# Rotary products read from PSUM, key-value latents three steps apart, top-k rounds moved to later stages: a layer with indexed sparse attention and latent attention on one core

## The chip, the core and the metric

The kernel runs on one core of one Trainium2 chip. The metric is the device time of one execution in microseconds. The core's engines run side by side and synchronize by semaphores: TensorE (PE, matrix products and transposes, which write the accumulator memory PSUM, eight banks of 128 rows by 512 fp32 columns), VectorE (DVE), ScalarE (ACT), GpSimd (POOL, which only works on SBUF here) and SyncE (SP, which issues the DMAs). Each engine works through its own queue in order: an instruction that waits holds up all that stand behind it on its engine.

## What is computed

One layer for 512 tokens of width 1024, in fp32:

```python
xn = rms_norm(h, norm_gain)
proj = xn @ w_in
(q_a, k_a, v_a, g_a, q_i, k_i, w_i, c_q, c_kv, k_rope, g_b) = split(proj)
# group A: 8 heads of 64; each query attends to 128 keys chosen by an indexer
q_i = [rope(q_i[..., :32]), q_i[..., 32:]]        # 8 index heads of 64
k_i = [rope(k_i[:, :32]), k_i[:, 32:]]            # one index key of 64
score[t, s] = sum_h w_i[t, h] * relu(q_i[t, h] . k_i[s]) * scale
sel = top_k(where(admissible, score, -1e30), 128)
o_a = softmax(rope(rms(q_a)) . rope(rms(k_a))[sel]) @ v_a[sel]
# group B: latent attention, 8 heads of 96
q_b = rms(c_q) @ w_uq
k_nope, v_b = split(rms(c_kv) @ w_ukv)
o_b = chunk_causal_softmax(rms(q_b), rms([k_nope, k_rope])) @ v_b
h = h + [o_a * silu(g_a), o_b * silu(g_b)] @ w_out
```

A query may read the keys of its own chunk of 64 tokens and of the chunks before it.

## The kernel before, in words

**Numbers as pairs.** Each matrix operand is a sum of a rounded high part and a low part. `mm3` (line 180) makes three matmuls of such pairs: high by high, low by high, high by low. One *step* of a projection is one `mm3` over 128 rows of the contraction, three matmuls of 512 columns.

**Order of the work.** PE's order is the order of the program (line 90); the other engines' queues are put in order when the kernel is built, by a planner with a cost model that prefers what comes earlier in the program among what it takes to be ready. A stage is a generator that yields after every step; `weave` (line 161) advances several of them in proportion to the numbers that it is given, and on a tie the one listed first. `later` (line 133) makes a function due a number of nanoseconds after now, by a clock of modelled matmul times (line 125), and `tick` starts what is due between two steps. `LAG_SMALL`, `LAG_QI` and `LAG_KI` are such numbers.

**Weights.** `wt` (line 275) has the pieces of the weights loaded eight ahead of use: a DMA into a buffer `wst` (three of them), the high part by ACT (line 267), the low part by POOL or DVE (line 270), into nine buffers each. `first` (line 226) keeps ACT's casts of weights beyond a number of pieces ahead behind a given instruction.

**Projections.** `tok_jobs` (line 291) and `feat_jobs` (line 301) make a list of jobs, one for each output tile; a job has `nk` steps into one PSUM bank and a function `use` that is called after its last step. `stream` (line 311) sets the order of the steps. Job i begins `nk / group` places behind job i - 1; with `skew` true it stays so, and with `skew` false its start is rounded down to a multiple of `nk`, so that with two jobs of eight steps in a group of two both start together, alternate, and end one after the other.

**The stages**, in order:

1. x is scaled, transposed and split (line 339), and the index keys, index weights and rotary key are projected (`small_step`, line 479). `use_small` (line 423) copies the result to SBUF; its `turn` transposes it into one PSUM bank `p`, ACT copies that to `sm` (line 431) and scales the index weights in it (line 432), DVE makes the two rotary products from `sm` (lines 438, 439), adds them twice (line 441) and copies the unrotated half twice (line 442); `turn2` transposes the keys and splits them into `KIH` and `KIL` (line 448, by `split`, line 416).
2. Index queries of token tiles 1, 2 and 3 (`qi_`, line 485). `use_qi` (line 503) copies the bank `a` to SBUF with ACT (line 507), DVE makes the rotary products from that copy (`rope_mul`, lines 410 and 413) and adds them in place (line 509); `turn` transposes and splits (lines 517, 520).
3. `lkv` (line 561): two key-value latents of eight steps. `latent` (line 455) takes squares and the high part with ACT (lines 460, 461) and the low part with DVE (line 462). The first nine steps run alone, the other seven are woven with five steps of `index` (line 531).
4. `lq`: three query latents, woven with the other 19 steps of `index`. A step of it makes one head's scores in a bank `sc` or `tr`, two of each, ACT applies relu in the bank (line 541), and DVE adds it, weighted, to `acc` (lines 544, 546), which frees the bank.
5. Top-k: `topk` (line 549) has 48 steps, 16 rounds for each of three token tiles. A step finds eight maxima (MAX8, line 554) and strikes them out (MATCH_REPLACE8, line 555), both on DVE, behind the DVE instruction last noted in `dve[0]`; after the 48th, three instructions (line 558) make masks. `TK` (line 64) says how many steps go with which stage: the end of `lq` (5), the first gates of group B (5), the first up-projection (5), the second (14), attention B (10), the stage with the projections of k_a (4); the last 5 go with the stage after that.
6. The up-projections `up(0)` and `up(1)` (line 671), each woven with 12 steps of gates. Their tiles use two banks `sc`; ACT evacuates (lines 637 to 639, 660, 661), and DVE's line 642 is the last reader of a key-value tile's bank.
7. Attention B (line 810) with the gate and q_a projections (line 874), the k_a projection, whose `use` ends with a product on DVE (line 831), and v_a.
8. Attention A (line 901), whose line 694 adds the masks to the scores and frees their bank, with the output projection.

Of the kernel before, what the change touches and what calls it, by code (L numbers as in the profile page):

```python
# [11 lines left out]
AF = mybir.ActivationFunctionType  # L12
# [5 lines left out]
NT = S // 128  # L18
# [38 lines left out]
KEEP_QI = 5  # L57
# [3 lines left out]
KEEP_EXP = 4  # L61
KEEP_UP = 4

TK = (5, 5, 5, 14, 10, 4)
I0, I1, I2 = 9, 5, 20
B1, B2, B3, B4 = 84, 23, 11, 7
A0, A1, OA = 2, 62, 18
# [17 lines left out]
def layer(ctx: ExitStack, tc: tile.TileContext, x, norm_gain, w_in, a_q_norm, a_k_norm, b_q_latent,  # L85
          b_kv_latent, w_uq, w_ukv, b_q_norm, b_k_norm, w_out, cst, out):
    nc = tc.nc
# [12 lines left out]
    def tmp(shape=(128, 512)):  # L100
        return sb("tmp", shape)
# [124 lines left out]
    def first(ins, m):  # L226

        for c in copies[used[0] + 1 + m:]:
            after(c, ins)
# [71 lines left out]
    def feat_jobs(name, nk, rh, rl, tiles, use):  # L301

        def job(c, m):
            def step(a, k):
                h, l = name(k) if callable(name) else wt(name, k)
                mm3(a[:m], h[:, c:c + m], l[:, c:c + m], rh(k), rl(k), k == 0, k == nk - 1)
            return nk, step, lambda a: use((c, m), a)

        return [job(c, m) for c, m in tiles]

    def stream(jobs, group=2, banks=("mm",), skew=True):

        order, start = [], 0
        for i, (nk, _, _) in enumerate(jobs):
            s = start if skew else start - start % nk
            order += [(s + k, i, k) for k in range(nk)]
            start += nk / group
        acc = {}
        for _, i, k in sorted(order):
            nk, step, use = jobs[i]  # L320
            if k == 0:
                acc[i] = psum(banks[i % len(banks)])
            step(acc[i], k)
            if k == nk - 1:
                use(acc.pop(i))
            yield 1
# [49 lines left out]
    cs32 = P.tile([128, 2, NT, 32], F32, name="cs32")  # L376
# [30 lines left out]
    def rope_mul(m1, m2, src, tab, t, heads, d):  # L407

        h = d // 2
        nc.vector.tensor_tensor(  # L410
            halves(m2), halves(src)[:, :, ::-1, :],
            tab[:, 1, t].rearrange("p (s d) -> p s d", s=2)[:, None].to_broadcast([128, heads, 2, h]), op=OP.mult)
        nc.vector.tensor_tensor(m1, src, tab[:, 0, t][:, None, :].to_broadcast([128, heads, d]), op=OP.mult)
# [5 lines left out]
    sm = P.tile([128, NT, 104], F32, name="sm")  # L419
# [3 lines left out]
    def use_small(_, a):  # L423
        st = tmp()
        nc.scalar.copy(st[:104], a[:104])

        def turn():
            p = psum("tr")
            for t in range(NT):
                transpose(p[:, t * 104:t * 104 + 104], st[:104, tok(t)], ident[:104, :104])  # L430
            nc.scalar.copy(sm.rearrange("p t c -> p (t c)"), p[:, :416])
            nc.scalar.activation(sm[:, :, 96:104], sm[:, :, 96:104], AF.Copy, scale=512 ** -0.5)

            kid = tmp((128, NT, 128))
            k4 = kid.rearrange("p t (u d) -> p t u d", u=2)
            m = tmp((128, 2, NT, 32))
            src = sm[:, :, 32:64]
            nc.vector.tensor_tensor(m[:, 0], src, cs32[:, 0], op=OP.mult)
            nc.vector.tensor_tensor(halves(m[:, 1]), halves(src)[:, :, ::-1, :], halves(cs32[:, 1]), op=OP.mult)
            for u in range(2):  # L440
                nc.vector.tensor_tensor(k4[:, :, u, 0:32], m[:, 0], m[:, 1], op=OP.add)
                nc.vector.tensor_copy(k4[:, :, u, 32:64], sm[:, :, 64:96])

            def turn2():
                p = psum("tr")
                for t in range(NT):
                    transpose(p[:, tok(t)], kid[:, t], ident)
                split(KIH, KIL, p)
            later(LAG_KI, turn2)
        later(LAG_SMALL, turn)  # L450
# [52 lines left out]
    def use_qi(t, a):  # L503
        q = tmp()
        q3 = q.rearrange("p (h d) -> p h d", h=8)
        m = tmp((128, 8, 32))
        first(nc.scalar.copy(q, a), KEEP_QI)
        rope_mul(q3[:, :, 0:32], m, q3[:, :, 0:32], cs32, t, 8, 32)
        nc.vector.tensor_tensor(q3[:, :, 0:32], q3[:, :, 0:32], m, op=OP.add)

        def turn():
            p = psum("tr")
            for h in range(4):
                transpose(p[:, tok(h)], q[:, tok(h)], ident)
            p3 = p.rearrange("p (h c) -> p h c", h=4)
            for u in range(2):
                nc.scalar.copy(QI[u][HALF[u], :, tok(t - 1)], p3[HALF[u]])
            for u in range(2):
                a, b = QI[u][HALF[u], :, tok(t - 1)], QI[u][HALF[1 - u], :, tok(t - 1)]
                nc.vector.tensor_tensor(b, p3[HALF[u]], f32(a), op=OP.subtract)  # L520
        later(LAG_QI, turn)
# [36 lines left out]
            nc.vector.tensor_scalar(masks[t], masks[t], -2e38, NEG, op0=OP.is_gt, op1=OP.mult)  # L558

    ix = index()  # L560
    lkv = stream(feat_jobs("c_kv", 8, xh, xl, [(0, 128), (128, 128)], lat_kv), 2, ("pv", "mm"), False)
    lq = stream(feat_jobs("c_q", 8, xh, xl, [(0, 128), (128, 128), (256, 128)], lat_q), 3, ("mm",), True)
    run(take(lkv, I0))
    weave((lkv, 16 - I0), (take(ix, I1), I1))
# [52 lines left out]
    src = sm[:, :, 0:32]  # L617
# [348 lines left out]
```

## Time and profile before

| | |
|---|---|
| median of 3 runs | 345.5 us (345.32 to 345.57) |
| the profiled execution | 345.63 us, span 343.8 us |
| PE busy | 326.7 us (95%) |
| DVE busy | 265.5 us (77%) |
| ACT busy | 219.6 us (64%) |
| POOL busy | 182.2 us (53%) |
| granted TensorE clock | 0.998 |

The profile is of one execution. Times are microseconds from the start of the span. A row of a timeline gives start, duration, engine, line, operation, the tiles out<-in, the shape and, in brackets, how long the engine had been idle before and which instruction's end released it. A row "x2" joins two instructions that follow each other. Matmuls are pipelined and overlap in the records, so PE's pace is read from start to start. A row of groups gives the count, the total busy time and the mean duration in nanoseconds; a row of one line's forms gives the least, median and greatest duration in nanoseconds, then the first and the last start; a row of a stretch gives its length and then the busy time of PE, of PE's weight loads, of DVE, ACT and POOL, the granted clock, and the DMA share and rate.

### The profile page before, as it was taken

The page shows a single profiled execution, that of the slowest core. Times are in us where ns is not written, and L with a number is a line of the kernel's source. Part 1 is how long each engine was busy: PE and PEld are TensorE (multiplying, and loading weights), DVE is VectorE, ACT ScalarE, POOL GpSimd, SP SyncE. Part 2 cuts the span into 40 slices and gives each one's busy share as a digit, 9 for nine tenths or more (in the row PEclk, how much of TensorE's full clock was granted, in tenths as well). Part 3 has the DMA queues.
Part 4 walks back from the last instruction along what each step waited for, and adds up shares of the span by engine and source line. Part 5 has one row for each costly group of instructions (what it writes and reads, how often), then busy time and mean ns, then how long its engine had stood idle before and what let it go on. Part 6 is the DMA issues. An engine that isn't in the chain of part 4 may idle for free.

```text
span 343.8 us, 5465 instructions
## 1 busy us (share of the span) xinstructions
PE 326.7 (95%) x1688; PEld 271.9 (79%) x1688; DVE 265.5 (77%) x634; ACT 219.6 (64%) x536; POOL 182.2 (53%) x193
## 2 busy tenths in 40 slices
PE   2999899999899999999999999999999999999995
PEld 2887787888688788788888788888888788788884
DVE  4925787759999797877779987679898776877466
ACT  4934558574757776878876898434526988878210
POOL 1745462166697998315623469519924635457100
PEclk9999999999999999999999999999999999999999
DMA  7753344124032433103320055515697324410006
GB/s 267 196 151 98 84 132 126 29 94 122 2 99 71 113 92 102 54 2 92 92 64 0 1 128 159 144 24 141 170 212 216 126 79 137 120 66 0 2 0 244
DMA packets 28806, 34.83 MB, mean 101 GB/s; under 512 B 5341, under 2 KB 16874, under 8 KB 28778
## 3 DMA queue, kind: packets, MB, share of 16 engines
q1 hardware_dynamic: 28202, 33.57, 34.7%
q10 hardware_dynamic: 576, 0.92, 0.7%
q8 instruction: 13, 0.21, 0.3%
q14 instruction: 15, 0.12, 0.1%
HBM read 27.14 MB, written 2.10 MB: 85 GB/s over the span
## 4 chain that ended last, share of the span: by engine, by line
PE 49%; DVE 17%; POOL 11%; DMA 8%; issue 6%; ACT 6%; SPq 1%; POOLq 0%; DVEq 0%; ACTq 0%
PE mm L126 28%; PE sc L126 7%; DMA wst<-in_w_in 7%; PE pv L126 6%; PE tr L130 5%; POOL wl L270 4%; POOL sml L216 4%; DVE acc L555 2%; DVE ob L923 2%; DVE m L554 2%; PE mm L130 2%; DVE z L694 2%; ACT wh L267 2%; ACT z L696 1%; DVE wl L270 1%
## 5 line engine op out<-in xcount | busy, mean ns | idle before, releaser
L270 POOL TENSOR_TENSOR wl<-wst,wh 128x512 fp32r<-128x512 f32 (+2 forms) x79 | 98.3, 1253 | 59.3 <-ACT wh L267 47.9
L267 ACT CAST wh<-wst 128x512 fp32r<-128x512 f32 (+2 forms) x89 | 50.9, 586 | 30.2 <-DMA wst<-in_w_in 22.0
L126 PE MATMUL mm<-wh,xh 128*128 128x512 f32 x120 | 50.2, 419 | 0.0
L126 PE MATMUL mm<-wl,xh 128*128 128x512 f32 x120 | 47.6, 397 | 0.2 <-POOL wl L270 0.2
L126 PE MATMUL mm<-wh,xl 128*128 128x512 f32 x120 | 47.4, 395 | 0.0
L216 POOL TENSOR_TENSOR sml<-sml,nhalf 128x4 f32<-128x4 f32 (+2 forms) x28 | 32.0, 1149 | 25.9 <-ACT sml L825 14.8
L696 ACT ACTIVATE z<-z,sml 128x256 f32<-128x256 f32 (+2 forms) x64 | 35.9, 561 | 11.1 <-DVE sml L694 10.0
L713 POOL TENSOR_SCALAR z<-z,sml 128x512 f32<-128x512 f32 (+2 forms) x32 | 18.2, 570 | 41.6 <-DVE sml L709 31.4
L126 PE MATMUL mm<-xh,wh 128*128 128x512 f32 x80 | 33.3, 417 | 0.0
L126 PE MATMUL mm<-xl,wh 128*128 128x512 f32 x80 | 31.7, 396 | 0.0
L126 PE MATMUL mm<-xh,wl 128*128 128x512 f32 x80 | 31.6, 395 | 0.0
L126 PEld LDWEIGHTS mm<-wh,xl 128*128 128x128 f32 x120 | 22.6, 188 | 5.3
L554 DVE MAX8 m<-acc 128x8 f32<-128x512 f32 (+2 forms) x48 | 26.3, 549 | 0.0
L555 DVE MATCH_REPLACE8 acc<-m,acc 128x512 f32<-128x512 f32 (+2 forms) x48 | 25.9, 540 | 0.0
L126 PEld LDWEIGHTS mm<-wl,xh 128*128 128x128 f32 x120 | 22.8, 190 | 3.5 <-POOL wl L270 0.5
L126 PEld LDWEIGHTS mm<-wh,xh 128*128 128x128 f32 x120 | 22.7, 189 | 3.0
L694 DVE CUSTOM_DVE_ANT_0 z<-sc,wide,nqb 128x512 f32<-128x512 f32 (+3 forms) x32 | 17.4, 543 | 6.4 <-PE sc L126 6.2
L416 DVE TENSOR_TENSOR pl<-tr,ph 128x512 fp32r<-128x512 f32 (+1 forms) x32 | 17.6, 551 | 5.9 <-ACT ph L416 5.6
L416 ACT CAST ph<-tr 128x512 fp32r<-128x512 f32 (+1 forms) x32 | 15.2, 474 | 8.0 <-PE tr L130 7.6
L126 PE MATMUL sc<-kl,bhl 96*128 96x512 f32 (+3 forms) x96 | 20.2, 322 | 0.0
L126 PEld LDWEIGHTS sc<-kl,bhl 96*128 96x128 f32 x96 | 16.6, 189 | 3.2 <-DVE bhl L794 0.3
L923 DVE TENSOR_TENSOR ob<-mm,ob 128x512 f32<-128x512 f32 (+1 forms) x25 | 16.5, 667 | 2.9 <-PE mm L126 2.6
(214 smaller groups left out, 884.6 us busy)
## 6 DMA issues: line engine op xcount, KB each, us to landing
wst<-in_w_in SPq DMA_DIRECT2D x48, 256.0 KB, 2.7
wst<-in_w_out SPq DMA_DIRECT2D x16, 256.0 KB, 2.9
xin<-in_x SPq DMA_DIRECT2D x4, 512.0 KB, 4.1
k_a<-tmp SPq DMA_DIRECT2D x16, 128.0 KB, 3.5
ob<-in_x SPq DMA_DIRECT2D x8, 256.0 KB, 4.5
wst<-in_w_in SPq DMA_DIRECT2D x8, 192.0 KB, 2.6
wst<-in_w_uq SPq DMA_DIRECT2D x6, 192.0 KB, 2.3
wst<-in_w_in SPq DMA_DIRECT2D x8, 128.0 KB, 2.1
```

The lines of the kernel that those rows point to most:

```text
L126: nc.tensor.matmul(o, l, r, start=start, stop=stop)
L130: nc.tensor.transpose(o, i, idn)
L216: nc.gpsimd.tensor_tensor(dst, src, nhalf[:, :src.shape[-1]], op=OP.pow)
L267: copies.append(nc.scalar.copy(h, st))
L270: i = E(eng).tensor_tensor(l, st, f32(h), op=OP.subtract)
L416: return nc.scalar.copy(h, p), nc.vector.tensor_tensor(l, p, f32(h), op=OP.subtract)
L554: nc.vector.max(m, masks[t])
L555: dve[0] = nc.vector.match_replace(masks[t], m, masks[t], -3e38).ins
L694: m = nc.vector.tensor_tensor_reduce(z, sc[:, :n], mask(t), nq(h, t), 3e38, OP.add, OP.min, r[:, i:i + 1])
L696: e = nc.scalar.activation(z, z, AF.Exp, bias=r[:, i:i + 1], scale=-1.0, accum_out=r[:, 2 + i:3 + i])
L713: nc.gpsimd.tensor_scalar(z, z, w, 0.0, op0=OP.mult, op1=OP.add)
L923: nc.vector.tensor_tensor(o, p[:, :n], o, op=OP.add)
```

## The change

- `TK`: the first and second up-projection take 4 and 9 top-k steps in place of 5 and 14, attention B takes 13 in place of 10, and the stage with k_a 7 in place of 4. The sum of the six numbers is 43 as before.
- `stream` takes a number for `skew`: then each job starts that many places behind the one before. `lkv` gets 3: its first latent ends with the 12th of 16 steps, the second with the 16th.
- Index keys: DVE's rotary products read the PSUM bank, ACT copies the unrotated half out of the same bank twice in place of DVE's copies, and the scaling of the index weights stands behind all that.
- Index queries: ACT copies only the unrotated half of each head, and `rope_mul` reads the PSUM bank.

```diff
-TK = (5, 5, 5, 14, 10, 4)
+TK = (5, 5, 4, 9, 13, 7)
...
-            start += nk / group
+            start += nk / group if skew in (True, False) else skew
...
             nc.scalar.copy(sm.rearrange("p t c -> p (t c)"), p[:, :416])
-            nc.scalar.activation(sm[:, :, 96:104], sm[:, :, 96:104], AF.Copy, scale=512 ** -0.5)
+            p3 = p[:, :416].rearrange("p (t c) -> p t c", t=NT)
...
-            src = sm[:, :, 32:64]
+            for u in range(2):
+                nc.scalar.copy(k4[:, :, u, 32:64], p3[:, :, 64:96])
+            src = p3[:, :, 32:64]
...
             for u in range(2):
                 nc.vector.tensor_tensor(k4[:, :, u, 0:32], m[:, 0], m[:, 1], op=OP.add)
-                nc.vector.tensor_copy(k4[:, :, u, 32:64], sm[:, :, 64:96])
+            nc.scalar.activation(sm[:, :, 96:104], sm[:, :, 96:104], AF.Copy, scale=512 ** -0.5)
...
-        first(nc.scalar.copy(q, a), KEEP_QI)
-        rope_mul(q3[:, :, 0:32], m, q3[:, :, 0:32], cs32, t, 8, 32)
+        a3 = a.rearrange("p (h d) -> p h d", h=8)
+        first(nc.scalar.copy(q3[:, :, 32:64], a3[:, :, 32:64]), KEEP_QI)
+        rope_mul(q3[:, :, 0:32], m, a3[:, :, 0:32], cs32, t, 8, 32)
...
-    lkv = stream(feat_jobs("c_kv", 8, xh, xl, [(0, 128), (128, 128)], lat_kv), 2, ("pv", "mm"), False)
+    lkv = stream(feat_jobs("c_kv", 8, xh, xl, [(0, 128), (128, 128)], lat_kv), 2, ("pv", "mm"), 3)
```

## The prediction

> **What bounds the kernel now.** I read the page first, then the timeline of the matrix engine (PE), then the timelines of VectorE (DVE), ScalarE (ACT) and GpSimd (POOL) around each place where PE stood still, and last the stretches by stage.
>
> ```profile
> span 343.8 us, 5465 instructions
> PE 326.7 (95%) x1688; PEld 271.9 (79%) x1688; DVE 265.5 (77%) x634; ACT 219.6 (64%) x536; POOL 182.2 (53%) x193
> L554 DVE MAX8 m<-acc 128x8 f32<-128x512 f32 (+2 forms) x48 | 26.3, 549 | 0.0
> L555 DVE MATCH_REPLACE8 acc<-m,acc 128x512 f32<-128x512 f32 (+2 forms) x48 | 25.9, 540 | 0.0
> ```
>
> PE is busy nearly throughout, so nothing can be won but the places where it stands. A top-k step costs DVE 549 + 540 = 1089 ns, 1.09 us. In PE's timeline:
>
> ```profile
> 33.50 0.40 PE L126 MATMUL mm<-wl,xh 128*128 128x512 f32 x1
> 33.74 0.39 PE L126 MATMUL mm<-wh,xl 128*128 128x512 f32 x1
> 35.07 0.63 PE L130 MATMUL tr<-ident,tmp 128*128 128x128 f32 x4 [0.94 <-DVE tmp L509]
> 42.47 0.65 PE L130 MATMUL tr<-ident,tmp 128*128 128x128 f32 x4 [0.29 <-DVE kil L416]
> 59.83 0.44 PE L126 MATMUL tr<-kih,qi 128*128 128x384 f32 x1 [0.77 <-DVE acc L546]
> 89.43 0.50 PE L126 MATMUL sc<-wh,lath 128*128 128x512 f32 x1 [0.31 <-DVE vb L642]
> 95.25 0.45 PE L126 MATMUL sc<-wh,lath 128*128 128x384 f32 x1 [1.39 <-DVE vb L642]
> 116.33 0.44 PE L126 MATMUL sc<-wh,lath 128*128 128x384 f32 x1 [0.28 <-DVE vb L642]
> 143.92 0.66 PE L130 MATMUL tr<-ident,z 128*128 128x128 f32 x4 [0.26 <-ACT z L715]
> 158.97 0.42 PE L130 MATMUL pv<-ident,qst 128*96 128x128 f32 x2 [0.19 <-DVE tmp L746]
> ```
>
> Matmuls of 512 columns start 0.23 us apart when nothing is late (33.50 to 33.74). The first stop therefore costs 35.07 - 33.74 - 0.23 = 1.10 us, 0.16 more than the idle time in its bracket (the pipeline fills again). I add 0.16 to the next five as well: 0.45, 0.93, 0.47, 1.55 and 0.44. These six stops, 4.94 us, lie in the stages that are edited, and each ends on DVE.
>
> **The change part by part. The rotary products.** What the stop at 35.07 waits for is this chain, on ACT and then on DVE:
>
> ```profile
> 30.22 0.50 ACT L431 COPY sm<-tr 128x416 f32<-128x416 f32 x1
> 31.19 0.58 ACT L507 COPY tmp<-mm 128x512 f32<-128x512 f32 x1
> 35.73 1.17 ACT L517 CAST qi<-tr 64x512 fp32r<-64x512 f32 x2 [2.04 <-PE tr L130]
> ```
>
> ```profile
> 30.76 0.53 DVE L438 TENSOR_TENSOR tmp<-sm,cs 128x128 f32<-128x128 f32 x1 [3.06 <-ACT sm L431]
> 31.41 0.91 DVE L442 COPY tmp<-sm 128x128 f32<-128x128 f32 x2
> 32.24 1.03 DVE L441 TENSOR_TENSOR tmp<-tmp 128x128 f32<-128x128 f32 x2
> 33.20 0.41 DVE L410 TENSOR_TENSOR tmp<-tmp,cs 128x256 f32<-128x256 f32 x1
> 36.94 1.39 DVE L520 TENSOR_TENSOR qi<-tr,qi 64x512 fp32r<-64x512 f32 x2 [2.01 <-ACT qi L517]
> 41.72 0.69 DVE L416 TENSOR_TENSOR kil<-tr,kih 128x512 fp32r<-128x512 f32 x1
> ```
>
> Reading PSUM directly doesn't free DVE from ACT. The first L520 subtracts rows 0 to 63 and needs only the first L517, yet both L520 start at 36.94, as the second L517 ends (35.73 + 1.17 = 36.90): an access of a PSUM bank by DVE is queued behind ACT's accesses ahead of it in the program. So L438 will wait for L431 and for the two new ACT copies of the keys. The price of such a copy out of PSUM, 128 columns wide:
>
> ```profile
> 83.90 0.27 ACT L589 ACTIVATE tmp<-tr 128x128 f32<-128x128 f32 x1
> ```
>
> Two copies of 0.27 after L431 (end 30.72), overlapping a little as ACT's instructions do, put L438 at about 31.1, 0.35 later than now. The two L442 leave DVE (0.83 from start to start), and L438 has one operand in PSUM, so that its 0.53 can come down to the 0.28 of this shape; that is 0.25 more. L410 then starts at 33.20 + 0.35 - 0.83 - 0.25 = 32.5, and the query's copy ahead of it, half as wide, now lasts between 0.27 and L507's 0.58 and ends before 32 even behind the two new ones. So L509 ends 0.7 earlier: gain 0.7 of the 1.10 (bounds: 0 if the new wait eats it, 1.10 if the planner draws the query's products ahead of the keys' sums). PE keeps its order and is dense behind, so the 0.7 stays. The key split L416, the wait at 42.47, stands on DVE behind the last of the three L413, at 39.8, which took 0.96. Products read from PSUM (mm) are never stretched like that, while those from SBUF are:
>
> ```profile
> L413 DVE TENSOR_TENSOR tmp<-mm,ta x8: 678/680/681, 184.6 to 247.4; 128x512 f32<-128x512 f32 x8
> L413 DVE TENSOR_TENSOR tmp<-tmp,cs x3: 424/426/961, 33.6 to 39.8; 128x256 f32<-128x256 f32 x3
> ```
>
> 0.96 - 0.43 = 0.53 is more than the stop: gain 0.4 (0 to 0.45). ACT's 0.5 of new copies lie ahead of the 2.04 that it idles before L517, and the scaling L432, moved behind them, feeds index scores far later: nothing for either. No DMA and no POOL instruction is added or moved past another.
>
> [...]
>
> **The latents.** The wait at 59.83 is for a score bank that DVE empties late, because ACT is late: both key-value latents end together (last two of 16 steps) and ACT does both squares and both casts between the score activations.
>
> ```profile
> 50.62 0.51 ACT L267 CAST wh<-wst 128x384 fp32r<-128x384 f32 x1 [1.61 <-DMA wst<-in_w_in]
> 55.08 0.58 ACT L460 ACTIVATE tmp<-pv 128x512 f32<-128x512 f32 x1
> 56.13 0.60 ACT L541 ACTIVATE sc<-sc 128x512 f32<-128x512 f32 x1
> ```
>
> One latent holds ACT from 55.08 to 56.13, 1.05 us. With a distance of three the first latent ends at step 12 of 16 instead of 15, into the 1.61 of idle time before 50.62. The chain to 59.83 gets 1.05 earlier, more than 0.93; I take 0.75, since the queues are planned anew (0 to 0.93). The weights are wanted up to three steps sooner. The last one, k = 7, is ready at 43.54 + 0.74 on POOL, and the twelfth step starts, by today's clock, at 48.78:
>
> ```profile
> 43.54 0.74 POOL L270 TENSOR_TENSOR wl<-wst,wh 128x256 fp32r<-128x256 f32 x1
> 48.78 0.40 PE L126 MATMUL mm<-xh,wh 128*128 128x512 f32 x1
> ```
>
> Even 1.1 earlier PE finds it 3.4 us old. Its buffers are held up to three steps (2.1 us) longer, with c_q's casts as the next users, which are not wanted before the latents end; nothing.
>
> **The top-k rounds.** Six steps leave the up-projections (1 and 5), three go into attention B, three into the stage with k_a.
>
> ```profile
> 84.00:107.00 23.00, 21.31 (x100) 17.73 (x99) 22.90 (x70) 13.43 (x44) 17.48 (x20) 1.00 0.18 52
> 107.00:129.00 22.00, 21.72 (x102) 18.12 (x101) 19.84 (x53) 17.35 (x47) 21.12 (x25) 1.00 0.36 96
> 129.00:213.00 84.00, 83.08 (x475) 70.20 (x474) 67.99 (x187) 66.44 (x168) 43.91 (x43) 1.00 0.26 68
> 229.00:245.00 16.00, 16.00 (x75) 12.95 (x74) 12.96 (x20) 7.44 (x14) 11.54 (x8) 1.00 0.58 141
> 245.00:259.00 14.00, 14.00 (x66) 11.36 (x65) 13.76 (x31) 4.86 (x10) 6.76 (x8) 1.00 0.79 191
> ```
>
> The third number behind the stretch's length is DVE's busy time. In the first up-projection DVE is full (22.90 of 23.0), mostly with rounds that were issued before it; there only one goes. The step just ahead of the evacuation that PE waits for at 95.25:
>
> ```profile
> 94.40 0.41 DVE L554 MAX8 m<-acc 128x8 f32<-128x256 f32 x1
> 94.74 0.46 DVE L642 SCALAR_TENSOR_TENSOR vb<-sc,rlx,vb 128x256 fp32r<-128x256 f32 x1
> ```
>
> With four steps its twelfth maximum is issued after the sixth up-projection step instead of after the fifth, so behind this evacuation: 94.74 - 94.40 = 0.35 gained of 1.55 (0 to 1.55); the 0.47 stays. In the second one 5 x 1.09 = 5.4 us go out of 19.84, and DVE is no longer late: the 0.44 goes (0 to 0.44). In attention B DVE goes from 67.99 to 71.3 of 84. Ten steps there were ahead of two stops of 0.26 + 0.19, so three more cost about 0.15; I take 0.2 (0 to 1.1, one whole step in PE's way). At the end DVE is full (13.76 of 14.0) and the masks are just in time for attention A:
>
> ```profile
> 261.71 0.73 DVE L694 CUSTOM_DVE_ANT_0 z<-sc,acc,nqa 128x512 f32<-128x512 f32 x1
> 264.40 0.28 PE L126 MATMUL sc<-k_a,q_a 128*128 128x256 f32 x1
> ```
>
> The third score needs the bank that L694 leaves at 262.44, so 2.0 us are to spare. By the order of issue one of the three steps falls before the third key tile's projection ends, into idle time, and two behind the last one: 2.2 us later, 0.2 over what is to spare; I take 0.3 (0 to 1.3, all three behind it).
>
> **Sum.** 0.7 + 0.4 + 0.75 + 0.35 + 0.44 - 0.2 - 0.3 = 2.1 us. The profiled execution took 345.63 (span 343.8, the rest around it), and the median of the runs is 0.13 lower: 345.5 - 2.1 = 343.4.
>
> **Rivals.** *All of the up-projection's wait goes* (0.12): the rest of the stop at 95.25 and that at 89.43, 1.2 + 0.47, vanish as the queue is planned anew: 341.7. For it: one step is enough to reorder a full queue. Against it: eight of ten older rounds still stand there.
>
> *ACT's copies keep DVE waiting* (0.20): neither rotary gain comes, 1.1 us: 344.5. For it: L520. Against it: L442 does leave DVE.
>
> *The head start is given back* (0.16): PE comes 1.85 us sooner to the up-projections, but DVE, full there, doesn't: 345.2. Against it: the rounds start behind c_q's latent, which comes as much earlier.
>
> *Slower* (0.12): all six moved steps end behind k_a's last product, 6.5 us later, with 2.0 to spare: PE waits 4.5 for the masks instead of 0.3; with the gains of 2.64 and the 0.2 it comes to 347.6. It decides from 4.6 us of lateness on. For it: that queue is full. Against it: attention B has 16 us of idle DVE time.
>
> **How the numbers follow.** The forecast has 0.40: 343.4, by itself from 342.2 (the other 1.2 us of the stop at 95.25 go too) to 344.4 (the 0.7 and the 0.35 don't come). The range 341.5 to 345.5 takes in both faster rivals (341.7, 344.5) and the head start given back (345.2), with 0.2 to 0.3 at either end. A measurement tells 0.2% (0.7 us) from no change: faster than 344.8 are forecast, first two rivals, 0.72 less 0.02 for their edges; the same is the third rival; slower the fourth and a little more: 0.70, 0.16, 0.14.
>
> **What would show it.** In the new profile: L438 starts right behind two short ACT copies, and PE's wait before the first query transposes is 0.4 or less; no wait for kil; none at the eighth or ninth index score; still a wait over 1 us for vb in the first up-projection, none in the second; L558's last one about 2 us later against attention A's first score. The forecast is wrong if DVE's wait for ACT is as long as now, or if PE waits over 1 us around the masks.

## The result, and the profile after

The changed kernel takes 343.53 us (median of 5 runs, 343.03 to 344.85), beside 345.57 us of the kernel before on the same chip (5 runs, 345.32 to 346.88): ratio 0.9939, 95% interval 0.9911 to 0.9967, so 2.0 us faster. The profiled run took 343.63 us. The head of its page:

```profile
span 341.7 us, 5466 instructions
PE 326.1 (95%) x1688; PEld 271.9 (80%) x1688; DVE 264.7 (77%) x632; ACT 219.1 (64%) x538; POOL 181.8 (53%) x193
```

The busy times hardly move; what moved are the places where PE stands. From line 440 on, a line of the changed kernel has a number two or three higher than in the kernel before: the queries' sum L509 is now L512, vb's L642 is L645, the masks' L558 is L561 and attention's L694 is L697. PE's timeline of the changed kernel, at the places that the prediction showed and three more:

```profile
19.43 0.50 PE L126 MATMUL mm<-wl,xh 128*128 128x512 f32 x1
...
35.02 0.63 PE L130 MATMUL tr<-ident,tmp 128*128 128x128 f32 x4 [0.77 <-DVE tmp L512]
...
40.42 0.63 PE L130 MATMUL tr<-ident,tmp 128*128 128x128 f32 x4
...
42.29 0.60 PE L130 MATMUL tr<-ident,tmp 128*128 128x128 f32 x4
...
58.66 0.34 PE L126 MATMUL tr<-kih,qi 128*128 128x384 f32 x1
...
88.15 0.50 PE L126 MATMUL sc<-wh,lath 128*128 128x512 f32 x1 [0.31 <-DVE vb L645]
...
93.66 0.45 PE L126 MATMUL sc<-wh,lath 128*128 128x384 f32 x1 [1.07 <-DVE vb L645]
...
114.03 0.33 PE L126 MATMUL sc<-wh,lath 128*128 128x384 f32 x1
...
139.43 0.50 PE L126 MATMUL sc<-kl,bhl 96*128 96x512 f32 x1 [0.89 <-DVE bhl L797]
...
193.21 0.63 PE L130 MATMUL tr<-ident,tmp 128*128 128x128 f32 x4 [0.39 <-DVE pl L416]
...
264.86 0.45 PE L126 MATMUL sc<-k_a,q_a 128*128 128x384 f32 x1 [0.18 <-DVE sml L697]
```

The brackets at 42.29, 58.66 and 114.03 are gone; the one at 35 is still there, the one at 93.66 is a little shorter, and two are new, at 139.43 and 264.86. Counted from start to start as in the prediction (the bracket and some 0.16), the five brackets here are 0.93, 0.48, 1.22, 1.04 and 0.35 us, leaving out the one at 193.21, which was there before. Of the prediction's list of signs, four came (L438's place taken by a product right behind two short ScalarE copies, no wait for kil, none at the index scores, over 1 us in the first up-projection and none in the second), and two didn't: the stop ahead of the query transposes is 0.93 and not 0.4, and the masks are not 2 us later. For the three added places, the rows of the kernel before:

```profile
19.32 0.50 PE L126 MATMUL mm<-wl,xh 128*128 128x512 f32 x1 [0.21 <-POOL wl L270]
...
195.53 0.63 PE L130 MATMUL tr<-ident,tmp 128*128 128x128 f32 x4 [0.48 <-DVE pl L416]
...
266.73 0.42 PE L126 MATMUL sc<-k_a,q_a 128*128 128x384 f32 x1
```

PE has the same 1688 instructions in all kernels of this study, and in the same order but for the steps of the two latents between 39 and 53 us, which the skew exchanges with each other. The landmarks below are the same instructions in every kernel, and as much work lies between them, so the length from one to the next measures a stretch without what lies ahead of it. The landmarks are the instructions that start, in the kernel before, at 19.32, 35.07 (first query transposes), 42.47 (transposes behind kil), 59.83 (index scores), 95.25 (first up-projection), 116.33 (second), 195.53 (attention B done) and 266.73 (the sixth score of attention A).

| stretch in us | before | after | predicted change | measured |
|---|---|---|---|---|
| A: 19.32 to 35.07 | 15.75 | 15.58 | -0.7 | -0.17 |
| B: to 42.47 | 7.40 | 7.27 | -0.4 | -0.13 |
| C: to 59.83 | 17.35 | 16.37 | -0.75 | -0.98 |
| D: to 95.25 | 35.43 | 35.00 | -0.35 | -0.43 |
| E: to 116.33 | 21.08 | 20.38 | -0.44 | -0.70 |
| F: to 195.53 | 79.20 | 79.17 | +0.2 | -0.03 |
| G: to 266.73 | 71.19 | 71.65 | +0.3 | +0.46 |

The sum is -1.98. PE started 0.11 later at the first landmark (19.43) and took 0.07 longer behind the last, so its last product ends 1.8 us earlier; the other 0.3 of the span lies behind that product.

How well a stretch repeats can be seen in the runs below. The latents' skew alone and the top-k steps alone leave the order of the kernel before on PE, VectorE, ScalarE and GpSimd as it is up to 39 us; A is 15.46 and 15.14 in them, beside 15.75. Four runs share the changed kernel's order up to there (the rotary part alone, the old distribution, and the two that move three steps): 15.85, 15.27, 15.45 and 15.55, beside 15.58. So A differs by up to 0.6 us between executions of one order, the two means are 15.45 and 15.54, and the -0.17 of the table is no measured gain. The stop moves as well. In three of these eight executions it stands ahead of the query transposes (0.94, 0.65 and 0.77); in the other five it stands near 26 us, for a weight's low part, as in the top-k steps alone and in the rotary part alone:

```profile
25.79 0.50 PE L126 MATMUL mm<-wl,xh 128*128 128x512 f32 x1 [0.23 <-POOL wl L270]
...
26.18 0.50 PE L126 MATMUL mm<-wl,xh 128*128 128x512 f32 x1 [0.86 <-POOL wl L270]
```

F differs by 0.6 us too (79.04 to 79.67 in the six runs with the old steps). B, C, D and E repeat within 0.25 us in the runs with three buffers where no edit bears on them, and G, with the old steps, is 71.14 to 71.20.

### The profile page after: what moved, and what is told of

It is laid out like the page before. It is cut to its first block, busy times and chain, and to the rows that moved or that the text cites. A ratio compares the mean times of both kernels' runs of the same rounds, so it can differ in the third digit from the quotient of the medians.

```text
span 341.7 us, 5466 instructions
## 1 busy us (share of the span) xinstructions
PE 326.1 (95%) x1688; PEld 271.9 (80%) x1688; DVE 264.7 (77%) x632; ACT 219.1 (64%) x538; POOL 181.8 (53%) x193
## 4 chain that ended last, share of the span: by engine, by line
PE 62%; DVE 18%; DMA 6%; POOL 4%; ACT 4%; issue 4%; SPq 1%; DVEq 0%; POOLq 0%; ACTq 0%
PE mm L126 34%; PE sc L126 11%; PE pv L126 8%; DMA wst<-in_w_in 5%; PE tr L130 5%; DVE acc L558 3%; DVE m L557 3%; PE tr L126 2%; POOL sml L216 2%; DVE ob L926 2%; PE mm L130 2%; DVE z L697 2%; ACT wh L267 1%; DMA xin<-in_x 1%; POOL wl L270 1%
## 5 line engine op out<-in xcount | busy, mean ns | idle before, releaser
L270 POOL TENSOR_TENSOR wl<-wst,wh 128x512 fp32r<-128x512 f32 (+2 forms) x79 | 97.1, 1239 | 50.6 <-ACT wh L267 50.3
L216 POOL TENSOR_TENSOR sml<-sml,nhalf 128x4 f32<-128x4 f32 (+2 forms) x28 | 33.1, 1185 | 25.0 <-ACT sml L828 13.6
L558 DVE MATCH_REPLACE8 acc<-m,acc 128x512 f32<-128x512 f32 (+2 forms) x48 | 25.9, 540 | 0.0
L697 DVE CUSTOM_DVE_ANT_0 z<-sc,wide,nqb 128x512 f32<-128x512 f32 (+3 forms) x32 | 17.3, 540 | 1.6 <-PE sc L126 1.6
```

Of the source, the lines that this page charges most:

```text
L216: nc.gpsimd.tensor_tensor(dst, src, nhalf[:, :src.shape[-1]], op=OP.pow)
L270: i = E(eng).tensor_tensor(l, st, f32(h), op=OP.subtract)
L558: dve[0] = nc.vector.match_replace(masks[t], m, masks[t], -3e38).ins
L697: m = nc.vector.tensor_tensor_reduce(z, sc[:, :n], mask(t), nq(h, t), 3e38, OP.add, OP.min, r[:, i:i + 1])
```

## The experiments

Each ran beside the kernel before on the same chip; "ratio" is to that kernel. Letters are the stretches above, of the profiled run. First each part alone.

**The rotary part alone**, on the kernel before: keys and queries.

```diff
...
+            for u in range(2):
+                nc.scalar.copy(k4[:, :, u, 32:64], p3[:, :, 64:96])
-            src = sm[:, :, 32:64]
+            src = p3[:, :, 32:64]
...
-                nc.vector.tensor_copy(k4[:, :, u, 32:64], sm[:, :, 64:96])
...
-        first(nc.scalar.copy(q, a), KEEP_QI)
-        rope_mul(q3[:, :, 0:32], m, q3[:, :, 0:32], cs32, t, 8, 32)
+        a3 = a.rearrange("p (h d) -> p h d", h=8)
+        first(nc.scalar.copy(q3[:, :, 32:64], a3[:, :, 32:64]), KEEP_QI)
+        rope_mul(q3[:, :, 0:32], m, a3[:, :, 0:32], cs32, t, 8, 32)
```

> The rotary part alone on the kernel before. Theory (DVE's products still stand behind ACT's copies out of the same bank, and the sums that read SBUF twice are stretched while GpSimd subtracts): the stop before the first query transposes goes from 1.10 only to about 0.9 us, the wait for kil goes and leaves about 0.3 before the second query transposes; 0.3 us in all, 345.2. Rival (the part is worth the 1.1 us of the prediction and the whole change lost the rest elsewhere): a stop of 0.4 or less, 344.4.

Measured: 344.14 us (10 runs) beside 345.47, ratio 0.9958 (0.9939 to 0.9976). A 15.85, B 7.24, C 16.44. The head gained nothing in A; a stop stood at 25 us instead. But C became 0.91 us shorter, as if the latents had been moved too. The time is the rival's, yet not by the rival's road: the part is worth about what the prediction gave it, 1.1 us, at another place.

**The latents' skew alone.**

```diff
-            start += nk / group
+            start += nk / group if skew in (True, False) else skew
...
-    lkv = stream(feat_jobs("c_kv", 8, xh, xl, [(0, 128), (128, 128)], lat_kv), 2, ("pv", "mm"), False)
+    lkv = stream(feat_jobs("c_kv", 8, xh, xl, [(0, 128), (128, 128)], lat_kv), 2, ("pv", "mm"), 3)
```

> The latents three steps apart alone on the kernel before. Theory (ACT's squares and casts of two latents at once made the score bank late): the stop at the ninth index score goes from 0.93 to 0, nothing else changes, 0.9 us, 344.6. Rival (the head start from the rotary part removed that stop): it stays at 0.5 or more, 345.0 or above.

Measured: 344.14 us (12 runs) beside 345.47, ratio 0.9963 (0.9945 to 0.998). C 16.48, 0.87 shorter than before; B 7.39, D 35.31, E 21.09 as before. This is the predicted place and size.

**The top-k steps alone.**

```diff
-TK = (5, 5, 5, 14, 10, 4)
+TK = (5, 5, 4, 9, 13, 7)
```

> The moved top-k steps alone on the kernel before. Theory: the stop of 1.55 us in the first up-projection goes to 1.2, the 0.6 of the second to 0; attention B and the masks give back 0.3 to 0.6 us: 344.9 to 345.2. Rival (the parts don't add: the steps gain only behind a head start): no change in the up-projections, 345.5 or above.

Measured: 344.73 us (12 runs) beside 345.47, ratio 0.9977 (0.9959 to 0.9995). D 35.11, E 20.37, F 79.01, G 71.57: -0.32, -0.71, -0.19, +0.38. The theory holds in both up-projections and at the masks. The stretch A, which this edit doesn't touch, was 15.14, the shortest of all with three weight buffers.

The three alone gain 1.33 + 1.33 + 0.74 = 3.4 us, all together 2.0. The stop in C is the overlap: the first two parts each remove it, and there is only one. It is 0.9 of the missing 1.4 us; the rest lies within the intervals.

**VectorE's products ahead of ScalarE's copies**, in the changed kernel, to test the rival that they wait for each other at the PSUM bank.

```diff
-            nc.scalar.copy(sm.rearrange("p t c -> p (t c)"), p[:, :416])
...
-            for u in range(2):
-                nc.scalar.copy(k4[:, :, u, 32:64], p3[:, :, 64:96])
             src = p3[:, :, 32:64]
             nc.vector.tensor_tensor(m[:, 0], src, cs32[:, 0], op=OP.mult)
             nc.vector.tensor_tensor(halves(m[:, 1]), halves(src)[:, :, ::-1, :], halves(cs32[:, 1]), op=OP.mult)
+            nc.scalar.copy(sm.rearrange("p t c -> p (t c)"), p[:, :416])
+            for u in range(2):
+                nc.scalar.copy(k4[:, :, u, 32:64], p3[:, :, 64:96])
```

(and the queries' copy behind `rope_mul` in the same way).

> The changed kernel with DVE's rotary products ahead of ACT's copies in the program, for keys and queries. Theory (accesses of one PSUM bank are queued in the order of the program): the first product starts as the transposes end, about 28.5 us instead of 31.1, the sums are done long before they are wanted, the stop of 0.93 us before the first query transposes goes and the one of 0.29 too: 342.4 to 342.8. Rival (the products were not held up by ACT's copies but by something else, the weights' DMA or DVE's own queue): they start at 31 as now and the stop stays, 343.5.

Measured: 343.52 us (6 runs) beside 345.47, ratio 0.993 (0.9904 to 0.9956); the changed kernel's is 0.9939. VectorE's first product does start earlier, as the transposes end and no longer as ScalarE's copies do, and in this run no stop stands ahead of the query transposes:

```profile
29.52 0.29 DVE L437 TENSOR_TENSOR tmp<-tr,cs 128x128 f32<-128x128 f32 x1 [2.66 <-PE tr L130]
```

In the changed kernel the same row (L440) stood at 31.14. Yet PE is at the query transposes at 34.95, hardly earlier than with the copies ahead (35.02): it stood 0.54 us at 25 us, for a weight's low part. Where the stop stands says nothing of this edit, since the four runs that share the changed kernel's order in A have it there too. The 0.29 us stop at the second query transposes is gone as expected (B 6.92), but C is 16.76, 0.39 longer, with a new wait for a score bank. The wait of VectorE at the bank is real, but without it no time is won that the measurement can tell.

**The old top-k distribution in the changed kernel.**

```diff
-TK = (5, 5, 4, 9, 13, 7)
+TK = (5, 5, 5, 14, 10, 4)
```

> The changed kernel with the old distribution of the top-k steps: rotary and latents' skew alone, together. If the steps' distribution is worth what it brought alone (345.47 - 344.73 = 0.74 us), and the three parts overlap only in the one stop at the index scores, this takes 343.5 + 0.7 = 344.2 us: the stops of the two up-projections come back (1.55 in place of 1.22 us in the first, about 0.6 in the second), the 1.04 us stop at attention B's 138 us falls to about 0.4, and the masks end as far ahead of attention A's first score as before. Rival: with the head start the maxima have less to wait for, and the distribution is worth nothing here: 343.5 us.

Measured: 344.73 us (6 runs) beside 346.34, ratio 0.9943 (0.9922 to 0.9965). D 35.33, E 21.10, F 79.52, G 71.14 against the changed kernel's 35.00, 20.38, 79.17, 71.65: the distribution gains 0.33 + 0.72 + 0.35 and gives back 0.51, 0.9 us in all. Of that the 1.05 of D and E repeats in other runs; F's 0.35 is within its scatter. The times don't settle it. Beside the run with the distribution and the ScalarE copies moved, on the same chip (343.88, below), this one is 0.85 us slower; but by the ratios to the kernel before, 0.9943 and the changed kernel's 0.9939, the difference is 0.1 us, far inside the intervals. That the distribution is worth its 0.74 us here too is likely by the stretches, and not shown by the times.

**Three older steps moved behind the first up-projection.**

```diff
-TK = (5, 5, 4, 9, 13, 7)
+TK = (5, 2, 4, 12, 13, 7)
```

> The changed kernel with three steps of the top-k moved from the gates' stage on to the second up-projection (5, 2, 4, 12, 13, 7), so that fewer stand in VectorE's queue ahead of the first up-projection's evictions. If older maxima ahead of L645 make the 1.22 us stop at 92 us, it falls below 0.7 us and the one at 87 us to under 0.2, while the second up-projection gets back 0.2 to 0.4 us: 343.0 to 343.4 us. Rival: the stop stands because L650, with both inputs in SBUF, is stretched from 0.41 to 1.18 us while GpSimd subtracts (and L645 is right behind it): the stop stays at 1.1 to 1.3 us, and the time is 343.5 to 343.9 us.

Measured: 343.63 us (6 runs) beside 346.34, ratio 0.9914 (0.9892 to 0.9937). D 34.57, 0.43 shorter than in the changed kernel; the stop at 93 fell from 1.22 to 0.81, not below 0.7, and the one at 88 stayed at 0.47. E 20.32: nothing came back. The rows of VectorE and GpSimd ahead of that stop, the changed kernel:

```profile
92.03 1.18 DVE L650 TENSOR_TENSOR kst<-kst,sml 128x256 f32<-128x256 f32 x1
93.13 0.47 DVE L645 SCALAR_TENSOR_TENSOR vb<-sc,rlx,vb 128x256 fp32r<-128x256 f32 x1
```

```profile
91.64 3.97 POOL L270 TENSOR_TENSOR wl<-wst,wh 128x512 fp32r<-128x512 f32 x3
```

and this run:

```profile
91.30 0.41 DVE L650 TENSOR_TENSOR kst<-kst,sml 128x256 f32<-128x256 f32 x1
...
92.50 0.46 DVE L645 SCALAR_TENSOR_TENSOR vb<-sc,rlx,vb 128x256 fp32r<-128x256 f32 x1
```

```profile
91.41 3.95 POOL L270 TENSOR_TENSOR wl<-wst,wh 128x512 fp32r<-128x512 f32 x3
```

Both theories hold a part. L650 has both inputs in SBUF; it takes 0.41 us when it starts before GpSimd's subtraction (91.30 against 91.41) and 1.18 when it starts behind it (92.03 against 91.64). Less old work ahead of it moved it in front. The rest of the stop, 0.81, is still there. And G grew to 72.30, which took 0.65 us back (see the masks, below); F, at 78.61, was 0.56 shorter, about its scatter.

**Three steps moved from attention B back to the second up-projection.**

```diff
-TK = (5, 5, 4, 9, 13, 7)
+TK = (5, 5, 4, 12, 10, 7)
```

> The changed kernel with three steps moved from attention B back to the second up-projection (5, 5, 4, 12, 10, 7). If attention B's three extra steps make its 1.04 us stop at 138 us (L797 waits behind a MAX8), the stop falls to 0.4 us, and 0.2 to 0.4 us come back in the second up-projection: 343.0 to 343.5 us, with stage attention B 0.6 us shorter. Rival: the stop comes from L797's place behind the gate's L607 and L697 and not from the number of maxima: it stays at about 1 us, and the time is 343.7 to 343.9 us.

Measured: 344.18 us (6 runs) beside 346.34, ratio 0.9933 (0.991 to 0.9955). The 1.04 us stop at 139 is gone, and the rows show why; VectorE in the changed kernel, then in this run:

```profile
138.31 0.69 DVE L557 MAX8 m<-acc 128x8 f32<-128x512 f32 x1
138.92 0.46 DVE L797 SCALAR_TENSOR_TENSOR bhl<-tr,gcol,bhl 96x256 fp32r<-96x256 f32 x1
```

```profile
137.99 0.48 DVE L797 SCALAR_TENSOR_TENSOR bhl<-tr,gcol,bhl 96x256 fp32r<-96x256 f32 x1
...
139.90 0.69 DVE L557 MAX8 m<-acc 128x8 f32<-128x512 f32 x1
```

The maximum that stood ahead of L797 now stands behind it. But F is 79.15, the changed kernel's 79.17: small stops at 141 and 156 us (0.43 and 0.35 from start to start, both there in the kernel before) came back. E is 20.39: the second up-projection takes the three steps for nothing. So the mechanism of that stop was right and its price, 0.6 us, was wrong. G grew by 0.31, to 71.96.

**A weight cast behind the small turn's copies**, in the changed kernel.

```diff
-            nc.scalar.copy(sm.rearrange("p t c -> p (t c)"), p[:, :416])
+            first(nc.scalar.copy(sm.rearrange("p t c -> p (t c)"), p[:, :416]), 2)
...
-                nc.scalar.copy(k4[:, :, u, 32:64], p3[:, :, 64:96])
+                first(nc.scalar.copy(k4[:, :, u, 32:64], p3[:, :, 64:96]), 2)
```

> The changed kernel with the three ScalarE copies of the small turn (L431, L438 twice) put ahead of one weight cast L267 that stood in front of them and waited for its transfer until 29.97 us. If that cast is what ate the rotary part's gain, the copies start at about 28.8 us, VectorE's first product near 29.7 instead of 31.14 us, the 0.93 us stop ahead of the first query transposes falls to 0.3 us or less, and PE stands 0.5 to 0.9 us earlier at the first index score transposes; of this 0.2 to 0.6 us reaches the end: 342.9 to 343.3 us. Rival: the cast moved behind the copies makes PE wait for its weight, or the head start is given back at the index scores, where casts of c_q's weights set the pace: 343.4 to 343.7 us.

Measured: 343.88 us (6 runs) beside 346.34, ratio 0.9922 (0.99 to 0.9944). No stop stands ahead of the query transposes, and A is 15.79, no shorter than the changed kernel's 15.58. PE's row that has it instead:

```profile
26.82 0.50 PE L126 MATMUL mm<-wl,xh 128*128 128x512 f32 x1 [0.86 <-POOL wl L270]
```

The theory of the one cast falls: A didn't get shorter, and PE loses as much earlier, for a weight, as it does in the four runs that share the changed kernel's order in A.

**A fourth buffer for arriving weights**, in the changed kernel. In all runs so far A was between 15.14 and 15.85 us, whichever edits they had, and the stop stood now at 25, now at 34 us. What its weights' transfers wait for, ahead of 36 us in the changed kernel (us in total, times, longest):

```profile
SPq L263 <- POOL wl L270: 9.7, 9, 2.0
```

Each of nine transfers is issued only when GpSimd has done with a buffer.

```diff
-    "wst": 3, "wh": 9,
+    "wst": 4, "wh": 8,
```

> The changed kernel with four buffers for arriving weights in place of three (one of the nine for their upper halves is given up, so that it fits). In every run so far PE reaches the first query transposes between 34.8 and 35.5 us, whether the stop stands there (0.93 us) or at 25 us (0.4 to 1.1 us), and each transfer is issued only when GpSimd's subtraction has freed one of the three. If that ring sets the pace of the head, a fourth buffer takes the stops at 25 and 34 us away together (under 0.3 us left), PE reaches the transposes near 34.2 us and the first index score transposes 0.6 to 0.9 us earlier than in the changed kernel; at the end 342.9 to 343.3 us. Rival: GpSimd or the transfer itself sets the pace, and 35 us stays within 0.3 us: 343.4 to 343.8 us. (The planner reorders later work too, which may cost or bring 0.5 us there: the head is read apart.)

Measured: 343.05 us (6 runs) beside 345.8, ratio 0.9915 (0.9896 to 0.9933). Both stops are gone together:

```profile
34.20 0.60 PE L130 MATMUL tr<-ident,tmp 128*128 128x128 f32 x4
```

A is 14.65, which is the kernel before's 15.75 less its 1.10 us stop: nothing is left to win there. (ScalarE's queue also has one weight cast behind the small turn's copies here, as in the run before this one; by itself that didn't shorten A.) B and C are 7.23 and 16.43, like the changed kernel's, so the 0.8 us stays up to 59.83. Behind it G, at 72.55, gives 0.9 us back and E, at 20.67, 0.3, while F is 0.56 shorter. The gain of the whole over the changed kernel, 0.8 us by the ratios, is less than their intervals; what is shown is A, 14.65 here and in the next run against 15.14 to 15.85 in the twelve with three buffers.

**That and the earlier rounds together**: the fourth buffer, and `TK = (5, 2, 4, 12, 13, 7)`.

> Four buffers for arriving weights, and the top-k steps as in the run with three moved from the gates' stage to the second up-projection (5, 2, 4, 12, 13, 7). If both of its gains hold and add, the head is 0.6 us shorter than the changed kernel's and the stop at 92 us is 0.8 in place of 1.22 us: 342.3 to 342.9 us. Rival: what is won ahead of it is given back at attention A's first score, where the masks come late (its stop grew to 1.09 us when PE came 1.2 us earlier): 343.0 to 343.5 us.

Measured: 342.56 us (6 runs, 342.08 to 344.12) beside 345.8, ratio 0.991 (0.9886 to 0.9934): the fastest of the study by its median. A 14.65, D 34.57, E 20.34; PE is at attention A's projection (195.53 before) at 191.31, 1.9 us ahead of the changed kernel, and of that 0.76 is lost in G (72.41 against 71.65). The gain over the changed kernel, about 0.3% by the two ratios, is less than their intervals.

**The keys' half of the rotary part alone**, on the kernel before, and **the queries' half alone**. Two questions were left: where kil's wait comes from, and why the rotary part empties C.

```diff
-        first(nc.scalar.copy(q, a), KEEP_QI)
-        rope_mul(q3[:, :, 0:32], m, q3[:, :, 0:32], cs32, t, 8, 32)
+        a3 = a.rearrange("p (h d) -> p h d", h=8)
+        first(nc.scalar.copy(q3[:, :, 32:64], a3[:, :, 32:64]), KEEP_QI)
+        rope_mul(q3[:, :, 0:32], m, a3[:, :, 0:32], cs32, t, 8, 32)
```

is the queries' half; the keys' half is the rest of the rotary part's diff above.

> The kernel before with the index keys' half of the rotary part alone (products from PSUM, ScalarE's copies; the queries' product, the skew and the top-k steps as before). The prediction gave this half the 0.45 us wait for kil and nothing at the index scores: 0.45 us gone at 42 us, the 0.93 us stop at the index scores stays at 0.8 to 1.0 us, 345.0 to 345.2 us on a day when the kernel before takes 345.5. If the earlier keys are what lets ScalarE reach the index scores' relus in time, that stop goes too: 344.2 us, as with the whole rotary part.

Measured: 346.28 us (12 runs) beside 345.8, ratio 1.0012 (0.9996 to 1.0029). Neither stop went:

```profile
44.26 0.66 PE L130 MATMUL tr<-ident,tmp 128*128 128x128 f32 x4 [0.28 <-DVE kil L416]
...
61.79 0.45 PE L126 MATMUL tr<-kih,qi 128*128 128x384 f32 x1 [0.78 <-DVE acc L548]
```

(this profiled run was 2.0 us late by the first landmark already; B and C, 7.36 and 17.52, don't hang on that). The first theory was wrong on kil, and the rival on the scores.

> The kernel before with the index queries' half of the rotary part alone (products from the projection's PSUM bank, ScalarE copying half as much; the keys' products, the skew and the top-k steps as before). With the keys' half alone the 0.44 us wait for kil and the 0.95 us stop at the index scores both stayed, and its time was that of the kernel before (ratio 1.0012). If the queries' half carries the whole rotary part, both stops go here: kil under 0.1, index scores under 0.2, and the ratio is 0.995 to 0.998, like that of the whole part (0.9958). Rival: only both halves together bring VectorE to kil early enough, and the kil wait keeps 0.3 us or more: ratio 0.998 to 1.000.

Measured: 345.06 us (8 runs) beside 346.37, ratio 0.9958 (0.9939 to 0.9977), the same as for the whole part. Both stops are gone, B 7.24 and C 16.47:

```profile
42.59 0.60 PE L130 MATMUL tr<-ident,tmp 128*128 128x128 f32 x4
...
59.06 0.44 PE L126 MATMUL tr<-kih,qi 128*128 128x384 f32 x1
```

So the queries' half is the whole of the rotary part. For the scores its way, as far as the rows tell, is ScalarE's queue. ScalarE in this run around the second score's activation (L542 here, L541 before):

```profile
50.13 0.58 ACT L542 ACTIVATE tr<-tr 128x512 f32<-128x512 f32 x1
51.42 0.51 ACT L267 CAST wh<-wst 128x384 fp32r<-128x384 f32 x1 [0.72 <-DMA wst<-in_w_in]
```

In the kernel before the activation stood behind such a cast, which idled 1.61 us for its transfer (the row at 50.62 in the prediction). Here it stands ahead of it. The third activation, at 52.89, still stands behind casts that idled for their transfers, 0.72 and 0.53 us, but the longest wait, 1.61, is out of the way. That the halved copies moved the order is the planner's doing; why it put them so was not tried.

## Why the prediction was right, point by point

**The total was right, 343.4 us against 343.5, on errors that cancel; that they did is luck.** By the stretches, rotary brought 0.8 us less than written, in A and B; C, D, E and F brought 0.8 more (0.23 + 0.08 + 0.26 + 0.23); G cost 0.16 more, PE began 0.11 later, and 0.3 came behind its last product.

**The 0.7 us ahead of the query transposes didn't come**, and the failing step is "PE keeps its order and is dense behind, so the 0.7 stays". ScalarE and VectorE in the changed kernel:

```profile
29.97 0.41 ACT L267 CAST wh<-wst 128x256 fp32r<-128x256 f32 x1 [2.27 <-DMA wst<-in_w_in]
30.28 0.50 ACT L431 COPY sm<-tr 128x416 f32<-128x416 f32 x1
30.68 0.43 ACT L438 COPY tmp<-tr 128x128 f32<-128x128 f32 x2
```

```profile
31.14 0.29 DVE L440 TENSOR_TENSOR tmp<-tr,cs 128x128 f32<-128x128 f32 x1 [3.34 <-ACT tmp L438]
...
31.67 1.57 DVE L443 TENSOR_TENSOR tmp<-tmp 128x128 f32<-128x128 f32 x2
33.16 0.41 DVE L410 TENSOR_TENSOR tmp<-mm,cs 128x256 f32<-128x256 f32 x1
...
33.94 0.93 DVE L512 TENSOR_TENSOR tmp<-tmp 128x256 f32<-128x256 f32 x1
```

The first product starts at 31.14, right behind two ScalarE copies, as predicted (31.1). But the sums, both of whose inputs are in SBUF, took 1.57 and 0.93 where the kernel before has 1.03 and 0.83, so L410 is at 33.16 and not at 32.5. That alone is the smaller part: where the chain was quick (the order turned round, the cast moved), and in the four runs that share the changed kernel's order in A, PE was as late at 35, having stood at 25. The ring of three weight buffers holds PE to about that time, whether it stands here or there, and taking the chain away wins nothing. The fourth buffer showed it: A fell to 14.65. So the 0.7 was booked for a stop that the kernel before itself doesn't always have: in the run with the top-k steps alone it isn't there, with no part of the chain changed.

**kil's wait**: predicted 0.4 gone, and gone. The reason given, that the third L413 is no longer stretched (0.96 us before, 0.41 after), fits the queries' half, which does it alone. The landmark moved by only 0.13 because a new stop of 0.29 us came at the second query transposes (40.42), behind sums of 1.51 for two.

**The latents**: predicted 0.75, measured 0.98 in C, and 0.87 for the skew alone. In the changed kernel the cast still idles for its transfer, and the first latent's square follows it behind one score's activation, instead of at 55.08:

```profile
50.32 0.52 ACT L267 CAST wh<-wst 128x384 fp32r<-128x384 f32 x1 [1.43 <-DMA wst<-in_w_in]
...
51.26 0.58 ACT L462 ACTIVATE tmp<-pv 128x512 f32<-128x512 f32 x1
```

The mechanism is the one predicted. What the prediction missed is that another part of the change removes the same stop; it had put nothing of the rotary part there, and said only of the moved scaling that it "feeds index scores far later: nothing". It did no harm to the sum, since the sum counted the stop once.

**The up-projections**: 0.35 and 0.44 predicted, 0.43 and 0.70 measured. The stop at 95.25 went from 1.55 to 1.22, and the 0.44 went whole; the second also lost some 0.3 us at 111 us, too small to be listed. That older rounds make the rest of that stop was half the story: just ahead of it L650 takes 0.77 us longer when it starts behind a GpSimd subtraction (1.18 against 0.41), and the run in which it started before one lost 0.41 us less there.

**Attention B**: 0.2 predicted, nothing measured. The new 1.04 us stop at 139 comes, and smaller ones behind it go. Over all runs the sign was wrong too, if anything: F is 78.61 to 79.17 in the seven runs with 13 steps in attention B and 79.04 to 79.67 in the seven with 10, and in the run with the cast moved, where VectorE's order is the changed kernel's, the stop at 139 has a bracket of only 0.43.

**The masks**: 0.3 predicted, 0.46 measured, by another road. They were to end 2.2 us later against attention A's first score; in fact the last ends 0.42 later (2.81 us behind that score's start, before 2.39). The term that failed is the 2.0 us to spare. It was read at the third score, which runs without a wait in the changed kernel too. The sixth score needs the bank of the fourth, and VectorE left that at 266.65 in the kernel before, 0.08 ahead of the score's start at 266.73: nothing was to spare. VectorE's product on the fourth score, before and after:

```profile
266.31 0.34 DVE L694 CUSTOM_DVE_ANT_0 z<-sc,wide,nqa 128x128 f32<-128x128 f32 x1
264.45 0.34 DVE L697 CUSTOM_DVE_ANT_0 z<-sc,wide,nqa 128x128 f32<-128x128 f32 x1
```

So what the masks lose, PE loses. In all six runs with the old steps the last mask ends 2.39 us behind the first score's start. In the six with moved steps and three buffers it ends 2.75 to 3.51 behind it, and G grows by the same, within 0.05 us: by 0.38 to 1.11.

How long L561 takes is a part of that. VectorE and GpSimd in the changed kernel,

```profile
257.94 0.68 DVE L561 TENSOR_SCALAR acc<-acc 128x512 f32<-128x512 f32 x2
...
259.05 0.88 DVE L561 TENSOR_SCALAR acc<-acc 128x256 f32<-128x256 f32 x1
```

```profile
256.65 3.12 POOL L270 TENSOR_TENSOR wl<-wst,wh 128x512 fp32r<-128x512 f32 x2 [0.15 <-ACT wh L267]
```

and in the run with three steps moved from attention B:

```profile
257.82 1.77 DVE L561 TENSOR_SCALAR acc<-acc 128x512 f32<-128x512 f32 x2
...
260.02 0.29 DVE L561 TENSOR_SCALAR acc<-acc 128x256 f32<-128x256 f32 x1
```

```profile
255.19 4.18 POOL L270 TENSOR_TENSOR wl<-wst,wh 128x512 fp32r<-128x512 f32 x3 [7.16 <-DMA k_a<-tmp]
```

Two masks take 0.68 or 1.77 us and the small one 0.88 or 0.29, and they fall differently against GpSimd's subtractions. With four buffers and the earlier rounds they took longest:

```profile
255.31 2.39 DVE L561 TENSOR_SCALAR acc<-acc 128x512 f32<-128x512 f32 x2
...
258.68 0.79 DVE L561 TENSOR_SCALAR acc<-acc 128x256 f32<-128x256 f32 x1
```

There PE was 1.1 us earlier than in the changed kernel at attention A's sixth score after having been 1.9 ahead, with a stop of 1.11. That the masks' end sets the stop rests on the equality above; that GpSimd's subtractions make the masks late is read from the rows, and no run keeps the two apart.

**The rivals.** That all of the up-projection's wait goes fell (1.22 stays). That ScalarE's copies keep VectorE waiting came true in the head as a wait and not as a price: no gain came in A, as that rival said, but turning the order round removes the wait and the time is the same. The rows show the order of the program on that bank: VectorE starts at 31.14, behind ScalarE's copies, which end at 31.11, and with the order turned round it starts at 29.52, as the transposes end. What makes one engine wait for the other there, no run shows. The bound lay elsewhere. That the head start is given back was partly so, in G only. The slower rival fell: the masks' stop is 0.35 us, not 4.5. What it had right is that the masks could become PE's limit.

## What to carry to other kernels

A stop on the bounding engine names only the wait that ended last; before its cure is booked as a gain, ask how late the next condition would have been, here the ring of weight buffers, and look for the same loss to come up earlier in the queue. A stop seen in one execution may also be elsewhere in the next, with nothing changed: compare the stretch over several runs. Parts that each remove the same stop don't add: price stretches between fixed instructions, not single stops, and measure each part alone. Where every queue is planned anew, an edit's largest effect can lie in a stage that it doesn't touch, as the queries' half copy had in the index scores.

## What was not expected of the hardware

That a VectorE product from SBUF can be stretched was known from the prediction's rows (0.43 to 0.96). The runs put a GpSimd subtraction beside it. L650, two SBUF inputs, 256 columns: 0.41 or 1.18 us. L561, which has a single input: 0.35 to 1.45 us for 384 columns. The longest of these adds 1.1 us, less than the 1.3 us that one subtraction of 512 columns takes. The queries' products that read PSUM took 0.41 or 0.42 us, all six of them, the last one too, at 39.30, beside a GpSimd subtraction that had begun at 39.25. What lies behind the stretching, no run shows.
